# Down projections with seven block products for four of eleven 2x2 block groups, in a two-layer decoder trunk

## The chip, the cores and the metric

The kernel runs on one core of one Trainium2 chip. The metric is the device time of one execution in microseconds (us), lower is better. Each kernel is timed in several executions, and the median is given.

## What is computed

Two pre-norm decoder layers on 256 tokens of width 2048, all in float32: three groups of attention heads behind one input projection, an output projection `w_o`, and a gated MLP with a causal convolution. The change is in the MLP's last product:

```python
def _conv_gated_mlp(h, w_up, conv_w, conv_b, w_down):
    u = jnp.einsum('bsd,df->bsf', h, w_up)            # 2048 -> 2 x 5632
    u = lax.conv_general_dilated(u, conv_w[:, None, :], ...) + conv_b   # causal, width 3, per channel
    a, g = jnp.split(u, 2, axis=-1)
    return jnp.einsum('bsf,fd->bsd', jax.nn.silu(g) * a, w_down)        # 5632 -> 2048

for l in range(DEPTH):          # DEPTH = 2, D_FF = 5632, D_MODEL = 2048, SEQ = 256
    ...
    x = x + jnp.einsum('bsm,md->bsd', mix, w_o[l])
    h = _rmsnorm(x, ffn_norm[l])
    x = x + _conv_gated_mlp(h, ffn_w_up[l], ffn_conv_w[l], ffn_conv_b[l], ffn_w_down[l])
return _rmsnorm(x, final_norm)
```

## The kernel before

Every float32 value is split into two parts, `hi` (rounded to the format that TensorE multiplies fast) and `lo` (the rest), and a product is three matmuls: hi by hi, hi by lo, lo by hi.

**The weight stream.** All weights lie in HBM in the order in which they are used, as blocks of 128x128, 16 to a chunk (1 MB). `load` brings a chunk into one of three `raw` buffers with one DMA from the queue of SyncE. `convert(s)` turns half a chunk (eight blocks, 128x1024) into a `hi` tile, with a cast on ScalarE (line 140), and a `lo` tile, with a subtraction on VectorE (line 141). There are five `hi` and five `lo` buffers, so the conversion of a half-chunk waits until TensorE is done with the half-chunk five places earlier. `weights` calls `convert` for the half-chunk in use and the next two, the last with a higher priority (`AHEAD`, in places of program order).

**The MLP.** It runs in two halves of 22 column tiles of the inner width. For each tile the up projection makes two products over 16 blocks (`mm_t`, lines 195 and 200, each a PSUM bank of the three called `mm`), `total` adds the two parts of a bank (ScalarE line 269, VectorE line 271), and GpSimd, ScalarE and VectorE apply scale, convolution and gate (lines 834 to 842). `to_hl` splits the result into `hi` and `lo` in one `slot` tile (32 slots). Then `residual(acts, ...)` does the down projection of this half: for each of four column groups of 512 (`j`), `mm_v` goes over the 22 tiles; for each tile and each half of the 256 tokens (`t`) it issues three matmuls with the activations as the stationary operand (lines 251 to 253), and two `mm` banks collect the sums. At the end of a column group VectorE adds each bank to the residual `xr[t]` (line 471). In the second half of a layer the squares of the finished columns are summed on ScalarE (line 433) and, in layer 0, the columns are transposed on TensorE for the next layer (`RowNorm.turn`, line 442, PSUM banks `s`); in layer 1 GpSimd multiplies them by the final gain (line 863).

**What sets the order.** The queues of the engines are filled by a list scheduler when the program is built: it goes by priority (the order of the code, moved by `high_priority`) and by its own estimate of when operands are ready. At run time each queue is worked off in its order; an instruction that waits holds all behind it on its engine.

## Time and profile before

| | |
|---|---|
| median of 3 runs (lowest, highest) | 2248.11 us (2248.07, 2248.27) |
| the profiled execution, its own time | 2248.09 us |
| its span, from the first to the last instruction | 2246.3 us |
| granted TensorE clock, mean | 0.999 |
| TensorE busy | 2235.3 us, 12083 matmuls |
| VectorE, ScalarE, GpSimd busy | 1487.2, 1205.2, 404.3 us |
| weights and inputs read from HBM | 409.49 MB, 183 GB/s over the span |

In the profile, PE is TensorE, PEld its loading of stationary operands, DVE VectorE, ACT ScalarE, POOL GpSimd, SP the queue of SyncE. Matmuls are pipelined, so a matmul's recorded duration is longer than the time from one to the next. "idle before" is time in which an engine stood still ahead of an instruction, with the instruction that ended it.

### The profile page before, as it was taken

How to read it: one execution, taken by the hardware profiler on the slowest of the kernel's cores; microseconds unless marked ns; L12 is line 12 of the kernel's file. 1: busy time of each engine (PE TensorE's matmuls, PEld its weight loads, DVE VectorE, ACT ScalarE, POOL GpSimd, SP SyncE). 2: the span in 40 equal slices, each digit the busy share in tenths (PEclk: the TensorE clock that was granted, in tenths of full speed). 3: DMA queues.
4: the chain of work that ended last, by engine and by line, in shares of the span. 5: the costliest groups of instructions: out<-in, count | busy, mean ns of one | idle time of the engine just before them, and what ended most of it. 6: DMA issues, size and time to landing. Idle time of an engine off the chain costs nothing.

```text
span 2246.3 us, 31038 instructions
## 1 busy us (share of the span) xinstructions
PE 2235.3 (100%) x12083; PEld 1928.9 (86%) x12083; DVE 1487.2 (66%) x2318; ACT 1205.2 (54%) x1869; POOL 404.3 (18%) x395
## 2 busy tenths in 40 slices
PE   9999999999999999999999999999999999999998
PEld 8888978888888888888888889788888888888887
DVE  8767766677764577775574787566666646777654
ACT  7455645555543455554454566456555434555543
POOL 4600000222210022220040110003333101222210
PEclk9999999999999999999999999999999999999999
DMA  8544445455555555555555444354555555555653
GB/s 317 200 158 160 154 141 180 163 192 195 190 206 187 187 188 188 189 198 195 187 173 202 151 156 169 131 183 174 187 187 188 206 191 187 192 190 190 213 188 131
DMA packets 60915, 413.59 MB, mean 184 GB/s; under 512 B 6880, under 2 KB 7008, under 8 KB 11744
## 3 DMA queue, kind: packets, MB, share of 16 engines
q1 hardware_dynamic: 60336, 411.06, 51.8%
q8 instruction: 95, 1.56, 0.3%
q10 hardware_dynamic: 432, 0.55, 0.1%
q14 instruction: 52, 0.43, 0.1%
HBM read 409.49 MB, written 2.10 MB: 183 GB/s over the span
## 4 chain that ended last, share of the span: by engine, by line
PE 99%; ACT 1%; DMA 0%; DVE 0%; issue 0%; SPq 0%; ACTq 0%
PE mm L195 37%; PE mm L200 19%; PE mm L251 12%; PE mm L253 12%; PE mm L252 12%; PE s L483 2%; PE mm L234 1%; PE mm L776 1%; PE mm L777 1%; PE mm L778 1%; PE pv L515 1%; PE mm L232 0%; PE s L442 0%; PE misc L386 0%; PE pv L516 0%; ACT hi L140 0%
## 5 line engine op out<-in xcount | busy, mean ns | idle before, releaser
L141 DVE TENSOR_TENSOR lo<-raw,hi 128x1024 fp32r<-128x1024 f32 (+1 forms) x776 | 974.5, 1263 | 499.6 <-ACT hi L140 461.0
L140 ACT CAST hi<-raw 128x1024 fp32r<-128x1024 f32 (+1 forms) x776 | 800.6, 1039 | 475.7 <-PE mm L253 369.0
L195 PE MATMUL mm<-h,hi 128*128 128x512 f32 x3584 | 863.8, 392 | 0.0
L195 PEld LDWEIGHTS mm<-h,hi 128*128 128x128 f32 x3584 | 664.7, 188 | 135.5 <-ACT tmp L269 1.3
L200 PEld LDWEIGHTS mm<-h,lo 128*128 128x128 f32 x3584 | 460.6, 190 | 13.6
L200 PE MATMUL mm<-h,lo 128*128 128x256 f32 x3584 | 465.4, 283 | 0.0
L251 PE MATMUL mm<-hi,slot 128*128 128x512 f32 x992 | 387.8, 391 | 0.0
L253 PE MATMUL mm<-hi,slot 128*128 128x512 f32 x992 | 384.8, 388 | 0.0
L252 PE MATMUL mm<-lo,slot 128*128 128x512 f32 x992 | 384.7, 388 | 0.0
L834 POOL TENSOR_TENSOR tmp<-tmp,rstd 128x256 f32<-128x256 f32 x176 | 193.1, 1097 | 1037.9 <-DVE tmp L271 728.0
L837 ACT ACTIVATE tmp<-tmp,par 128x256 f32<-128x256 f32 x176 | 106.0, 602 | 311.6 <-POOL tmp L834 311.6
L251 PEld LDWEIGHTS mm<-hi,slot 128*128 128x128 f32 x992 | 186.3, 188 | 41.1 <-issue 4.0
L253 PEld LDWEIGHTS mm<-hi,slot 128*128 128x128 f32 x992 | 186.2, 188 | 38.5
L252 PEld LDWEIGHTS mm<-lo,slot 128*128 128x128 f32 x992 | 186.4, 188 | 36.8
L838 DVE SCALAR_TENSOR_TENSOR tmp<-tmp,par,tmp 128x255 f32<-128x255 f32 x176 | 84.5, 480 | 150.5 <-ACT tmp L837 150.5
L269 ACT COPY tmp<-mm 128x256 f32<-128x256 f32 (+1 forms) x233 | 85.7, 368 | 62.0 <-PE mm L195 34.0
L842 POOL TENSOR_TENSOR tmp<-tmp,tmp 128x256 f32<-128x256 f32 x88 | 75.5, 858 | 211.6 <-ACT tmp L841 209.3
L271 DVE TENSOR_TENSOR tmp<-mm,tmp 128x256 f32<-128x256 f32 (+1 forms) x233 | 97.3, 418 | 5.4 <-ACT tmp L269 5.1
L839 DVE SCALAR_TENSOR_TENSOR tmp<-tmp,par,tmp 128x254 f32<-128x254 f32 x176 | 85.0, 483 | 6.2
L841 ACT ACTIVATE tmp<-tmp 128x256 f32<-128x256 f32 x88 | 36.8, 418 | 61.7 <-DVE tmp L839 61.7
L251 PE MATMUL mm<-hi,h 128*128 128x512 f32 (+1 forms) x192 | 68.3, 356 | 0.0
L253 PE MATMUL mm<-hi,h 128*128 128x512 f32 (+1 forms) x192 | 67.9, 354 | 0.0
(196 smaller groups left out, 1469.8 us busy)
## 6 DMA issues: line engine op xcount, KB each, us to landing
raw<-in_w SPq DMA_DIRECT2D x381, 1024.0 KB, 4.8
raw<-in_w SPq DMA_DIRECT2D x14, 256.0 KB, 5.3
slot<-in_x SPq DMA_DIRECT2D x8, 256.0 KB, 5.1
x<-in_xn SPq DMA_DIRECT2D x2, 1024.0 KB, 10.9
out<-x SPq DMA_DIRECT2D x6, 256.0 KB, 2.6
slot<-in_fin SPq DMA_DIRECT2D x4, 256.0 KB, 6.2
out<-x ACTq DMA_DIRECT2D x2, 256.0 KB, 2.6
par<-in_par SPq DMA_DIRECT2D x1, 325.0 KB, 7.9
```

The lines of the kernel that those rows point to most:

```text
L140: nc.scalar.copy(hi[:, a], src[:, a])
L141: nc.vector.tensor_tensor(lo[:, a], src[:, a], f(hi[:, a]), ALU.subtract)
L195: nc.tensor.matmul(ps, ws[i][0], moving[i], start=(i == 0), stop=bool(flip and i == k - 1))
L200: nc.tensor.matmul(ps[:, :T], ws[i][1], moving[i][:, :T], start=False, stop=(not flip and i == k - 1))
L251: nc.tensor.matmul(ps[t][:, :n], s_hi, hi, start=(i == 0), stop=False)
L252: nc.tensor.matmul(ps[t][:, :n], s_hi, lo, start=False, stop=False)
L253: nc.tensor.matmul(ps[t][:, :n], s_lo, hi, start=False, stop=(i == k - 1))
L269: nc.scalar.copy(t[:rows], ps[:rows, T : 2 * T])
L271: nc.vector.tensor_tensor(u[:rows], ps[:rows, :T], t[:rows], ALU.add)
L834: nc.gpsimd.tensor_tensor(uu, u, rstd, ALU.mult)
L837: nc.scalar.activation(y, uu, AF.Identity, scale=q_[:, w + 2 : w + 3], bias=q_[:, w + 3 : w + 4])
L839: nc.vector.scalar_tensor_tensor(y[:, 2:], uu[:, : T - 2], q_[:, w : w + 1], y[:, 2:], ALU.mult, ALU.add)
```

## The change

The four column groups of a down projection are taken in pairs of groups (columns `c1`, `c2` of 512 each) and the 22 tiles in eleven pairs (`PAIRS`). For a pair of tiles the product is then a 2x2 by 2x2 product of blocks: two token halves by two tiles, and two tiles by two column groups. For the pairs 3, 6, 8 and 10 (`SEVEN`) it is computed with seven block products, by Strassen's identity in Winograd's form, and for the other seven pairs with eight as before. This is done for both pairs of column groups in the first half of each layer, and for the first pair in the second half: six passes over eleven pairs in all, called groups here. The second half's last two column groups stay as they were.

A chunk of a seven-product pair gives 3.5 half-chunks of converted weights where it gave 2: twelve of its blocks directly, and four sums of blocks, which `prepare` makes with three additions on VectorE (one of 128x1024, two of 128x512, buffers `sum`). The activations of such a pair are likewise combined (`seven_forms`: four subtractions and additions of 128x128 on GpSimd, then four splits instead of two). The products go to seven PSUM banks, with an eighth, `d`, for what only the eight-product pairs add to the second token half and `c2`. At the end of a group the banks are combined into the residual with eight VectorE instructions, one ScalarE copy and four GpSimd additions, where four VectorE additions stood. `step` now converts three half-chunks ahead instead of two, everywhere.

```diff
-AHEAD = 60
+AHEAD = 80
+PAIRS = HALF // 2
+SEVEN = (3, 6, 8, 10)
...
     def tmp():
-        return work.tile([P, T], F32, tag="tmp", name=nm("tmp"), bufs=15)
+        return work.tile([P, T], F32, tag="tmp", name=nm("tmp"), bufs=14)
...
+        if at in sevens:
+            bounds += [(c, 0, 4, 8), (c, 0, 12, 4), (c, 1, 0, 8), (c, 2, 0, 8)]
+        else:
+            bounds += [(c, 0, i, min(SUB, n - i)) for i in range(0, n, SUB)]
...
+    def prepare(s):
...
+        tc.keep_in_program_order(nc.vector.tensor_tensor(
+            t13.rearrange(g, q=2), r[:, 1024:2048].rearrange(g, q=2),
+            r[:, 0:512].rearrange(g, q=1).to_broadcast([P, 2, 512]), ALU.add,
+        ))
+        nc.vector.tensor_tensor(t24[:, :512], t13[:, :512], r[:, 1536:2048], ALU.add)
+        nc.vector.tensor_tensor(t24[:, 512:], t24[:, :512], r[:, 512:1024], ALU.add)
...
+        src = (sums[c][form - 1] if form else raws[c])[:, o : o + n * P]
...
+    def step(s):
+        convert(s)
+        convert(s + 1)
+        with tc.high_priority(offset=AHEAD):
+            convert(s + 2)
+            convert(s + 3)
+            load(bounds[s][0] + 1)
+            load(bounds[s][0] + 2)
+        return subs[s]
...
+    def down(acts, groups):
+        for g in range(groups):
...
+            tags = {"d": ("s", 2), 2: ("s", 2), 3: ("pt", 1), 4: ("pv", 1), 1: ("mm", 3), 5: ("mm", 3), 7: ("mm", 3), 6: ("misc", 1)}
...
+            def prod(m, x, w, last=False):
...
+                nc.tensor.matmul(banks[m], xh, hi, start=fresh, stop=False)
+                nc.tensor.matmul(banks[m], xh, lo, start=False, stop=False)
+                nc.tensor.matmul(banks[m], xl, hi, start=False, stop=last)
...
+                if p in SEVEN:
+                    last = p == SEVEN[-1]
+                    step(s)
+                    prod(2, part(a[0], 1), quad(s, 0), last)
+                    prod(1, part(a[0], 0), quad(s, 1), last)
+                    step(s + 1)
+                    prod(3, part(a[2], 1), quad(s + 1, 0), last)
+                    step(s + 2)
+                    prod(5, part(a[1], 0), quad(s + 2, 0), last)
+                    prod(7, part(a[2], 0), quad(s + 2, 1), last)
+                    step(s + 3)
+                    prod(6, part(a[1], 1), quad(s + 3, 0), last)
+                    prod(4, part(a[3], 1), quad(s + 3, 1), last)
+                else:
...     (two products each into "d", 3, 2 and 4)
+            add = nc.vector.tensor_tensor
+            with tc.high_priority(offset=AHEAD):
+                add(xr[1][:, c2], xr[1][:, c2], banks["d"], ALU.add)
+                u = slot()
+                nc.scalar.copy(u, banks[1])
+                add(xr[0][:, c1], xr[0][:, c1], banks[2], ALU.add)
+                add(xr[0][:, c2], xr[0][:, c2], banks[3], ALU.add)
+                nc.gpsimd.tensor_tensor(xr[0][:, c1], xr[0][:, c1], u, ALU.add)
+                v = slot()
+                add(v, banks[6], u, ALU.add)
+                add(u, banks[5], v, ALU.subtract)
+                add(v, banks[7], v, ALU.add)
+                nc.gpsimd.tensor_tensor(xr[0][:, c2], xr[0][:, c2], u, ALU.add)
+                add(u, banks[5], v, ALU.subtract)
+                nc.gpsimd.tensor_tensor(xr[1][:, c1], xr[1][:, c1], v, ALU.add)
+                add(xr[1][:, c1], xr[1][:, c1], banks[4], ALU.add)
+                nc.gpsimd.tensor_tensor(xr[1][:, c2], xr[1][:, c2], u, ALU.add)
...
+    def seven_forms(both):
...
+        sub = nc.gpsimd.tensor_tensor
+        sub(s1, x21, x22, ALU.subtract)
+        sub(s3, x11, x21, ALU.subtract)
+        sub(s2, s1, x11, ALU.subtract)
+        sub(s4, x12, s2, ALU.add)
...
             if half == 0:
-                residual(acts, 0)
+                residual(acts, 0, first=4)
             elif l < DEPTH - 1:
...
-                residual(acts, 0, norm.turn)
+                residual(acts, 0, norm.turn, first=2)
             else:
-                gf = [slot() for _ in range(4)]
+                gf = [big.tile([P, 2 * T], F32, tag=f"h{k}", name=nm("gf")) for k in range(4)]
...
-                residual(acts, 0, gain, 8)
+                residual(acts, 0, gain, 8, 2)
```

In the rows below, a number behind a name tells buffers of one kind apart; line numbers are those of the respective kernel. In the changed kernel line 182 is the subtraction of `convert`, line 323 that of `total`, lines 551 to 553 are the three matmuls of `prod`, and the lines of the group's end are 592 (bank `d`), 594 (the copy of bank 1 to `u`, on ScalarE), 595 and 596 (banks 2 and 3), 597 (GpSimd, `u` into `xr[0]`, `c1`), 599 (`v` from bank 6), 600 (`u` from bank 5), 601 (`v` from bank 7), 602 (GpSimd, `u` into `xr[0]`, `c2`), 603 (`u` from bank 5 again), 604 (GpSimd, `v` into `xr[1]`, `c1`), 605 (bank 4) and 606 (GpSimd, `u` into `xr[1]`, `c2`).

**Place A: between the two groups of a first half** (layer 0). VectorE before, at the end of the second column group; the `lo` tiles are the next column group's weights:

```order
L141 TENSOR_TENSOR lo_1303_6776<-raw_1297_6741,hi_1302_6775 128x1024
L141 TENSOR_TENSOR lo_1306_6794<-raw_1297_6741,hi_1305_6793 128x1024
L471 TENSOR_TENSOR x0_77<-x0_77,mm_1271_6583 128x512
L471 TENSOR_TENSOR x1_78<-x1_78,mm_1272_6584 128x512
L141 TENSOR_TENSOR lo_1308_6810<-raw_1304_6779,hi_1307_6809 128x1024
L141 TENSOR_TENSOR lo_1311_6828<-raw_1304_6779,hi_1310_6827 128x1024
```

VectorE now. `lo_1338` (ahead of these rows) is the last half-chunk of pair 10, `lo_1341` and `lo_1343` (also ahead) are those of the next group's pair 0, and the rows begin with pair 1's:

```order
L182 TENSOR_TENSOR lo_1345_6856<-raw_1339_6830,hi_1344_6855 128x1024
L182 TENSOR_TENSOR lo_1349_6881<-raw_1339_6830,hi_1348_6880 128x1024
L595 TENSOR_TENSOR x0_77<-x0_77,s_1266_6467 128x512
L596 TENSOR_TENSOR x0_77<-x0_77,pt_1263_6456 128x512
L599 TENSOR_TENSOR slot_1347_6871<-misc_1292_6590,slot_1346_6866 128x512
L182 TENSOR_TENSOR lo_1354_6901<-raw_1350_6884,hi_1353_6900 128x1024
L600 TENSOR_TENSOR slot_1346_6866<-mm_1288_6578,slot_1347_6871 128x512
L601 TENSOR_TENSOR slot_1347_6871<-mm_1289_6582,slot_1347_6871 128x512
L182 TENSOR_TENSOR lo_1358_6919<-raw_1350_6884,hi_1357_6918 128x1024
L603 TENSOR_TENSOR slot_1346_6866<-mm_1288_6578,slot_1347_6871 128x512
L605 TENSOR_TENSOR x1_78<-x1_78,pv_1267_6474 128x512
```

Two additions have become seven here (`d` was added earlier), with two conversions between them. TensorE before, over the same boundary: the next column group starts in two other banks at once.

```order
L252 MATMUL mm_1272_6584<-lo_1294_6722,slot_1240_6388 128x512
L253 MATMUL mm_1272_6584<-hi_1293_6721,slot_1240_6388 128x512
L251 MATMUL mm_1300_6773<-hi_1295_6737,slot_799_4057 128x512
L252 MATMUL mm_1300_6773<-lo_1296_6738,slot_799_4057 128x512
L253 MATMUL mm_1300_6773<-hi_1295_6737,slot_799_4057 128x512
```

TensorE now, 38 matmuls behind the group's last one; the third of these rows is the first matmul into bank 4 (`pv`) of the new group, and belongs to pair 0:

```order
L551 MATMUL s_1351_6886<-hi_1353_6900,slot_885_4505 128x512
L552 MATMUL s_1351_6886<-lo_1354_6901,slot_885_4505 128x512
L551 MATMUL pv_1356_6911<-hi_1342_6845,slot_801_4061 128x512
L552 MATMUL pv_1356_6911<-lo_1343_6846,slot_801_4061 128x512
L553 MATMUL pv_1356_6911<-hi_1342_6845,slot_801_4061 128x512
```

The scheduler has put other products of the pairs 0 to 2 ahead of those that go into bank 4.

**Place B: from the second group of a first half into the up projection of the second half.** VectorE before; `mm_1359` is the bank of the first product of the up projection:

```order
L141 TENSOR_TENSOR lo_1361_7157<-raw_1356_7123,hi_1360_7156 128x1024
L141 TENSOR_TENSOR lo_1364_7163<-raw_1356_7123,hi_1363_7162 128x1024
L471 TENSOR_TENSOR x0_77<-x0_77,mm_1330_6965 128x512
L471 TENSOR_TENSOR x1_78<-x1_78,mm_1331_6966 128x512
L141 TENSOR_TENSOR lo_1371_7210<-raw_1362_7160,hi_1370_7209 128x1024
L141 TENSOR_TENSOR lo_1374_7216<-raw_1362_7160,hi_1373_7215 128x1024
L271 TENSOR_TENSOR tmp_1366_7200<-mm_1359_7155,tmp_1365_7198 128x256
```

VectorE now; `mm_1437` is the bank of that first product. The second product of the up projection is written to the bank that line 601 reads here (`mm_1378`), and waits for it.

```order
L182 TENSOR_TENSOR lo_1439_7319<-raw_1428_7267,hi_1438_7318 128x1024
L182 TENSOR_TENSOR lo_1442_7325<-raw_1440_7322,hi_1441_7324 128x1024
L595 TENSOR_TENSOR x0_77<-x0_77,s_1355_6904 128x512
L596 TENSOR_TENSOR x0_77<-x0_77,pt_1352_6893 128x512
L599 TENSOR_TENSOR slot_1436_7308<-misc_1381_7027,slot_1435_7303 128x512
L600 TENSOR_TENSOR slot_1435_7303<-mm_1377_7015,slot_1436_7308 128x512
L182 TENSOR_TENSOR lo_1449_7372<-raw_1440_7322,hi_1448_7371 128x1024
L601 TENSOR_TENSOR slot_1436_7308<-mm_1378_7019,slot_1436_7308 128x512
L323 TENSOR_TENSOR tmp_1444_7362<-mm_1437_7317,tmp_1443_7360 128x256
L603 TENSOR_TENSOR slot_1435_7303<-mm_1377_7015,slot_1436_7308 128x512
L605 TENSOR_TENSOR x1_78<-x1_78,pv_1356_6911 128x512
```

The chain of the group's end now stands between the conversions and reaches past the first `total` of the up projection. On TensorE, outside the down projections, the order of the matmuls is the same as before.

More of the change, by code (lines that the diff above doesn't have):

```diff
@@ L64, in chunk_list, with seven_starts @@
     return out
+def seven_starts():
+    per = KT * 39 + 84 + 16 * KT + 3 * FT * KT
+    out = set()
+    for l in range(DEPTH):
+        for half in range(2):
+            at = l * per + KT * 39 + 84 + 16 * KT + half * 3 * HALF * KT + 2 * HALF * KT
+            out |= {at + (g * PAIRS + p) * CH for g in range(2 - half) for p in SEVEN}
+    return out
 @with_exitstack
@@ L130, in convert @@
             return
-        c, o, n = bounds[s]
+        c, form, o, n = bounds[s]
         load(c)
         o = o * P
-        src = raws[c][:, o : o + n * P]
+        src = (sums[c][form - 1] if form else raws[c])[:, o : o + n * P]
         hi = wpool.tile([P, SUB * P], F32R, tag="hi", name=nm("hi"), bufs=5)
@@ L148, in weights @@
         if o == 0:
-            convert(s)
-            convert(s + 1)
-            with tc.high_priority(offset=AHEAD):
-                convert(s + 2)
-                load(bounds[s][0] + 1)
-                load(bounds[s][0] + 2)
+            step(s)
         o *= P
@@ L275 @@
     cs = const.tile([P, C_W], F32, tag="cs", name="cs")
-    pint = work.tile([P, T], I32, tag="tmp", name="pint", bufs=15)
+    pint = work.tile([P, T], I32, tag="tmp", name="pint", bufs=14)
     xr = [big.tile([P, D], F32, tag=f"x{t}", name=f"x{t}") for t in range(2)]
@@ L464, in rows, with residual @@
             return rows
-    def residual(stat, every, after=None, lag=0):
-        for j in range(4):
+    def residual(stat, every, after=None, lag=0, first=0):
+        if first:
+            down(stat, first // 2)
+            if after:
+                for j in range(first):
+                    for t in range(2):
+                        norm.add(j, t)
+                    if j:
+                        after(j - 1)
+            flat = []
+            for p, a in enumerate(stat):
+                flat += [((a[0], 0), (a[3], 0)), ((a[0], 1), (a[3], 1))] if p in SEVEN else a
+            stat = flat
+        for j in range(first, 4):
             ps = mm_v(stat, 512, every, {2: (lambda: after(j - 1))} if after and j else {}, lag if j == 3 else 0)
@@ L821 @@
         for half in range(2):
-            acts = []
+            acts, waiting = [], []
             for i in range(HALF):
```

109 lines of the change are left out of this document (99 added, 10 removed).

## Prediction

> **What bounds the kernel now.** I read the page first, then the chain that ended last, TensorE's own waits, and the stages one by one. On the page's busy row TensorE is busy for the whole span; in the row of the chain, 99% of it is TensorE; in the view of waits, TensorE's list is three entries of about a microsecond. The windows are the down projection of layer 0's first half, that of layer 1's first half, and the end.
>
> ```profile
> PE 2235.3 (100%) x12083; PEld 1928.9 (86%) x12083; DVE 1487.2 (66%) x2318; ACT 1205.2 (54%) x1869; POOL 404.3 (18%) x395
> PE 99%; ACT 1%; DMA 0%; DVE 0%; issue 0%; SPq 0%; ACTq 0%
> PE pv L284 <- DVE small L286: 1.5, 1, 1.5
> PE mm L231 <- DVE h L407: 0.8, 1, 0.8
> PE misc L371 <- DVE slot L559: 0.8, 1, 0.8
> 638.00:760.00 122.00, 122.00 (x547) 101.36 (x546) 63.01 (x59) 48.85 (x50) 1.85 (x2) 1.00 0.57 200
> 1753.00:1873.00 120.00, 120.00 (x531) 99.38 (x530) 62.87 (x61) 49.29 (x51) 4.40 (x3) 1.00 0.56 201
> 2240.00:2247.00 7.00, 0.00 (x0) 0.00 (x0) 1.31 (x3) 1.74 (x3) 0.00 (x0) 0.53 0.40 150
> ```
>
> In a down projection TensorE never stands still (122.00 of 122.00), VectorE works half of the time (63.01), GpSimd hardly. So the time is the sum of the matmuls' slots, and the question is twofold: how many slots go, and what new waits TensorE gets. The slot is not the recorded duration (0.39 us), which overlaps the next. From two starts in the timeline, 33 matmuls apart, it is (2237.45 - 2229.97) / 33 = 0.2267 us:
>
> ```profile
> 2229.97 0.39 PE L251 MATMUL mm<-hi,slot 128*128 128x512 f32 x1
> 2237.45 0.39 PE L251 MATMUL mm<-hi,slot 128*128 128x512 f32 x1
> ```
>
> **What goes.** Six groups, four pairs each, one block product of three matmuls less: 72 matmuls x 0.2267 = 16.3 us. All of it lies on the path. An eight-product pair takes 24 x 0.2267 = 5.44 us, a seven-product pair 4.76, a group 252 x 0.2267 = 57.1.
>
> **What comes, and its prices.** Groups by line and form, then the timeline for what instructions cost in a row and against each other:
>
> ```profile
> L141 DVE TENSOR_TENSOR lo<-raw,hi 128x1024 fp32r<-128x1024 f32 x762 | 964.9, 1274 | 495.5 <-ACT hi L140 457.0 <-PE mm L200 36.8 <-issue 0.4
> L141 DVE TENSOR_TENSOR lo<-raw,hi 128x512 fp32r<-128x512 f32 x14 | 9.5, 687 | 4.0 <-ACT hi L140 4.0
> L140 ACT CAST hi<-raw 128x1024 fp32r<-128x1024 f32 x762 | 792.2, 1047 | 470.0 <-PE mm L253 369.0 <-PE mm L195 56.9 <-issue 20.3
> L352 DVE TENSOR_TENSOR slot<-slot,sinT 128x512 f32<-128x512 f32 x8 | 5.5, 692 | 0.5
> L354 DVE TENSOR_TENSOR slot<-slot,slot 128x512 f32<-128x512 f32 x8 | 5.5, 689 | 0.2
> L671 ACT ACTIVATE slot<-mm,rcol 128x512 f32<-128x512 f32 x12 | 8.0, 686 | 3.9 <-PE mm L253 3.9
> L521 DVE TENSOR_TENSOR slot<-tmp,slot 128x256 fp32r<-128x256 f32 x96 | 40.2, 419 | 28.2 <-ACT slot L520 28.2
> L842 POOL TENSOR_TENSOR tmp<-tmp,tmp 128x256 f32<-128x256 f32 x88 | 75.5, 858 | 211.6 <-ACT tmp L841 209.3 <-issue 2.3
> L863 POOL TENSOR_TENSOR x<-x,slot x6: 1289/1501/1712, 2150.3 to 2211.8; 128x512 f32<-128x512 f32 x6
> 695.50 1.22 DVE L141 TENSOR_TENSOR lo<-raw,hi 128x1024 fp32r<-128x1024 f32 x1 [1.49 <-ACT hi L140]
> 696.64 1.28 DVE L471 TENSOR_TENSOR x<-x,mm 128x512 f32<-128x512 f32 x2
> 1026.38 0.39 PE L253 MATMUL mm<-hi,slot 128*128 128x512 f32 x1
> 1026.81 1.05 ACT L140 CAST hi<-raw 128x1024 fp32r<-128x1024 f32 x1 [1.67 <-PE mm L253]
> 1027.89 1.23 DVE L141 TENSOR_TENSOR lo<-raw,hi 128x1024 fp32r<-128x1024 f32 x1 [1.50 <-ACT hi L140]
> 2150.32 2.97 POOL L863 TENSOR_TENSOR x<-x,slot 128x512 f32<-128x512 f32 x2 [26.04 <-ACT slot L433]
> 2152.42 1.95 DVE L141 TENSOR_TENSOR lo<-raw,hi 128x1024 fp32r<-128x1024 f32 x1 [1.54 <-ACT hi L140]
> 411.67 0.74 POOL L842 TENSOR_TENSOR tmp<-tmp,tmp 128x256 f32<-128x256 f32 x1 [3.61 <-ACT tmp L841]
> 411.82 0.42 DVE L271 TENSOR_TENSOR tmp<-mm,tmp 128x256 f32<-128x256 f32 x1 [0.92 <-ACT tmp L269]
> 790.58 1.92 PE mm L200 x16
> raw<-in_w SPq DMA_DIRECT2D x381, 1024.0 KB, 4.8
> ```
>
> A conversion lasts 1.23 us undisturbed, but the next VectorE instruction that depends on nothing begins 1.14 later (695.50 to 696.64); two PSUM additions last 1.28 together, so one lasts 0.68 and its place in the queue is 0.60. From a matmul's start to the cast that it releases go 0.43 us, which is 0.20 past its slot; then 1.05 for the cast and 0.03 to the subtraction. GpSimd's 128x512 addition: 1.29 alone. Against GpSimd, a VectorE instruction with two SBUF operands is held: the conversion at 2152.42 ended 1.08 us after GpSimd did (2154.37 against 2153.29). One that reads PSUM and SBUF is not: 411.82 took its usual 0.42 while GpSimd ran. I take it that GpSimd likewise waits for a conversion that has begun, and needs 1.1 more.
>
> *The sums of weights.* No row has a 128x1024 addition with a repeated operand. Nearest: line 141, 1.23, and line 352, which repeats an operand and costs the same as line 354, which doesn't (692 and 689 ns). I take 1.14 in the queue, and 0.61 for each addition of 512. A seven-product chunk then costs VectorE 3 x 1.14 + 0.61 + 1.14 + 2 x 0.61 = 6.4 us against TensorE's 4.76, a plain one 2.28 against 5.44. So VectorE falls behind by 1.6 in each seven-product pair and gains 3.2 in each plain one; over a group it needs 4 x 6.4 + 7 x 2.28 + 8 x 0.60 = 46.4 of 57.1 us. The five buffers carry the swing: stepping through pairs 8, 9 and 10 (below), the last half-chunk of pair 10 is ready 1.7 us before its use. Inside a group I cost the sums at nothing; that cover is gone if the three together cost 1.7 us more than these 2.4. ScalarE's 3.5 casts are 3.7 us, below TensorE's 4.76. Loads land in 4.8; each is issued at least 5.4 ahead.
>
> *The forms of activations.* In the up projection, 16 pairs get two more splits (2 x 0.42 on VectorE, 2 x 0.41 on ScalarE) and four small GpSimd operations (each below line 842's 858 ns). TensorE waits there for conversions alone, which run four half-chunks (11 us) ahead; nothing on the path. Pair 10's forms hold the conversions of pair 3 behind them, for a chain some 2 us longer than today's; by my count these are ready 9 us into the down projection, and wanted at 16.3.
>
> *Fourteen `tmp` buffers, the gain's loads, three half-chunks ahead.* One buffer of fifteen; the gain's DMA now waits on SP for the last up projection, with one weight load behind it that isn't due for 10 us: nothing.
>
> **The ends of the groups** are what remains. Let T be the slot behind the group's last matmul. VectorE's queue is determined from pair 9 on: the second conversion of that pair needs the buffer of pair 8's first two products, done at T - 4.76 - 5.44 - 4.76 + 1.36 = T - 13.6; with 0.20, 1.05 and 0.03 behind it, it starts at T - 12.3. Then come, with the prices above, pair 10's two conversions, the sum, line 592, the sum, a conversion, the sum, and 1.1 us of waiting for ScalarE's cast of that sum. `lo_1338` (and its like) starts at T - 4.1, the next three at -3.0, -1.8 and -0.7; the fourth at +0.8, since ScalarE copies bank 1 ahead of its cast. TensorE has these in time.
>
> *Place A, twice.* Line 595 starts at 1.9 and ends at 2.6, while TensorE wants bank 2 at 10 slots, 2.3: a wait of 0.4. Lines 596 and 599 to 3.8. GpSimd runs line 597 from 2.7 to 3.95 and holds `lo_1354`, which ends at 5.0. Line 600 to 5.6, 601 to 6.35. Line 602 on GpSimd, 5.7 to 6.95, holds `lo_1358` to 8.0, and that holds line 604 to 9.1. Line 605 ends at 9.9. TensorE reaches bank 4 after 38 slots, at 8.6. Sum: 1.3 us. Without any holding 0.4; with the full 1.23 and 0.68 for each place in the queue, and GpSimd's additions at 1.5, 3.0.
>
> *Place B, twice.* Here two conversions stand ahead of line 595 (3.1) and one between 600 and 601. Line 597 runs on GpSimd from 3.8 to 5.1; 600 to 5.8; `lo_1449` to 6.95; 601 to 7.55. The second product of the up projection wants that bank at 5.58 (16 x 0.2267 and the 16 narrower ones, 1.92 in the chain: 5.55). A wait of 2.0. From below 1.5; if GpSimd gets ahead of `lo_1449` and everything lasts its full time, 4.35.
>
> *Second half of layer 0, once.* Seven matmuls behind T, TensorE transposes columns of `c1`, which wait for line 597, at 2.5 against 1.6: 0.9 us, and later 0.1 for line 605. 1.0; bounds 0.5 and 2.5. *Of layer 1, once:* the third bank is wanted after 27 slots, 6.1; the final gain's GpSimd multiplication stands between lines 597 and 602 and delays line 601 to 6.4. 0.3; bounds 0 and 1.7.
>
> Sum: 2 x 1.3 + 2 x 2.0 + 1.0 + 0.3 = 7.9 us; from below 2 x 0.4 + 2 x 1.5 + 0.5 = 4.3, from above 2 x 3.0 + 2 x 4.35 + 2.5 + 1.7 = 18.9. I take 7.9, the value by the prices in a row, which the timeline shows for this very sequence.
>
> **The forecast.** The profiled execution took 2248.09 us (span 2246.3; the median, 2248.11, is the same within 0.02). 2248.09 - 16.3 + 7.9 = 2239.7 us, 0.37% faster; with the bounds of the waits 2236.1 and 2250.7. A measurement of this kernel can tell 0.2%, 4.5 us, from no change.
>
> **The rivals.**
>
> *The ends take most of the gain* (no change). The same mechanism with waits of 12 to 20 us: each wait hangs on a queue, so a delay that I missed ahead of T moves all six. For it: 1.5 us more at each end is enough (7.9 + 9 = 16.9, 2248.7). Against it: in the trace VectorE's starts follow these prices to 0.05 us. Chance 0.22.
>
> *The sums are dear* (slower). If the three additions cost 4.7 instead of 2.4 us a chunk, pair 10's come out 2.35 later, and so does every step behind T in all six groups: 7.9 + 6 x 2.35 = 22, 2253.8 us. It decides against the change from waits of 16.3, that is 1.4 us more a chunk, and shows as slower from 20.8, 2.15 more. For it: no row of that form. Against it: lines 352 and 354. Chance 0.07.
>
> *TensorE loses its speed in the waits.* At its start it is slow: eleven matmuls of zeros take 4.31 us, 0.39 each instead of 0.2267, 1.8 us lost.
>
> ```profile
> 1.45 4.31 PE L284 MATMUL pv<-slot 128*128 128x512 f32 x11 [1.45 <-DVE small L286]
> 0.00:12.00 12.00, 9.74 (x42) 7.86 (x43) 7.06 (x16) 8.62 (x18) 2.87 (x9) 1.00 0.82 286
> ```
>
> If each of the two waits at place B did that again, the time would be 2239.7 + 3.6 = 2243.3; if all six did, 2250.5. The granted clock in the window's row is 1.00 even in that first stretch, so it can't tell. The Trainium skill ("TensorE: Matmul & The Clock Gate", Part 1) has a rule that speaks against the change here: TensorE's clock falls to half after an idle window of about 3.4 us and comes back after one such window of work. By that rule none of my waits, at most 2.0 us in one piece, is long enough, and the sum stays 7.9. No run here yet shows a wait in the middle. Chance 0.04.
>
> *Fewer matmuls don't show.* The order has the 72 fewer, with the same three into one bank at a time; the slot can't change by more than it does between today's stages. Left out.
>
> **How the numbers follow.** Forecast, waits between 4 and 12 us: 0.67, all faster than 2243.8. Ends take it: 0.22, of which 0.04 end over +0.2%. Sums dear: 0.07, mostly slower. Clock: 0.04, half of it faster. So faster 0.68, same 0.22, slower 0.10. The range must leave out no more than 0.2: from 2235 (waits of 3) to 2250 (waits of 18). The forecast's own is 2236 to 2244.
>
> **What the profile after would show.** 72 matmuls less at an unchanged slot. TensorE's list of waits with `pv` for line 605 (about 1 us, twice), `mm` of the up projection for line 601 (2 us, twice), `s` for lines 595 and 597 (below 1), 8 us in all, each wait at a group's end. VectorE about 135 us busier (24 x 4.5, and the ends). No wait of TensorE for a `lo` tile inside a group: such waits would speak for dear sums. Wrong I would be above all if the queue of VectorE comes to T later than I count.

## The result, and the profile after

The changed kernel takes 2262.78 us (median of 4 runs, 2259.59 to 2266.26) against 2248.09 us (2248.01 to 2248.27) for the kernel before: ratio 1.0065, 95% interval 1.0053 to 1.0077. It is slower by 14.7 us. The forecast was 2239.7 us, the range 2235 to 2250. The profiled execution took 2264.71 us, its span is 2262.9 us.

From the page of the changed kernel, the busy row and the chain that ended last:

```profile
PE 2232.6 (99%) x12011; PEld 1921.7 (85%) x12011; DVE 1625.9 (72%) x2494; ACT 1247.8 (55%) x1955; POOL 470.9 (21%) x483
PE 55%; DVE 8%; ACT 3%; issue 2%; POOL 2%; ACTq 0%; DVEq 0%; POOLq 0%
```

The 72 matmuls are gone (12083 to 12011), yet TensorE is busy only 2.7 us less, and the chain, which was TensorE for 99%, now runs through VectorE, ScalarE and GpSimd too. TensorE's waits in the changed kernel (us in total, times, longest):

```profile
PE mm L248 <- DVE lo L182: 6.9, 7, 1.7
PE mm L243 <- DVE slot L601: 3.6, 2, 1.8
PE mm L551 <- ACT hi L181: 1.9, 2, 1.0
PE mm L552 <- DVE lo L182: 1.9, 2, 1.0
PE pv L551 <- DVE x L605: 1.6, 2, 0.8
...
PE s L494 <- POOL x L597: 1.0, 1, 1.0
...
PE pv L648 <- DVE tmp L881: 0.7, 1, 0.7
PE pv L648 <- ACT slot L643: 0.7, 1, 0.7
...
PE misc L423 <- DVE tmp L890: 0.6, 1, 0.6
PE mm L304 <- DVE lo L182: 0.3, 1, 0.3
```

Four kinds can be told apart. `slot` for line 601, `x` for 605 and 597, and line 304 are the groups' ends (line 304 stands behind the last group of layer 1, and waits for a converted half-chunk). Line 248 is the up projection, which waits for converted weights. Lines 551 and 552 wait for the first seven-product pair of a group. Lines 648 and 423 are in the attention, far from the change's products. And there is something that is no wait. The windows of the down projection and, inside it, of two stretches of 4 us (the eighth column from the start of a row is the granted clock):

```profile
640.00:760.00 120.00, 117.25 (x515) 96.05 (x514) 96.85 (x105) 60.72 (x71) 13.08 (x13) 0.99 0.55 194
667.00:671.00 4.00, 3.75 (x9) 2.96 (x10) 3.97 (x5) 3.98 (x5) 0.00 (x0) 0.57 0.75 264
672.00:676.00 4.00, 4.00 (x19) 3.31 (x18) 3.08 (x4) 1.35 (x2) 0.00 (x0) 1.00 0.95 369
```

From 667 to 671 the clock is 0.57 and 9 matmuls are done where 19 are done a little later. TensorE's timeline there:

```profile
664.47 0.39 PE L553 MATMUL pt<-hi,slot 128*128 128x512 f32 x1
665.79 0.50 PE L551 MATMUL mm<-hi,slot 128*128 128x512 f32 x1 [0.94 <-ACT hi L181]
667.25 0.75 PE L552 MATMUL mm<-lo,slot 128*128 128x512 f32 x1 [0.95 <-DVE lo L182]
...
668.23 0.63 PE L551 MATMUL mm<-hi,slot 128*128 128x512 f32 x1
668.65 0.63 PE L552 MATMUL mm<-lo,slot 128*128 128x512 f32 x1
...
670.77 0.39 PE L551 MATMUL pv<-hi,slot 128*128 128x512 f32 x1
671.00 0.40 PE L552 MATMUL pv<-lo,slot 128*128 128x512 f32 x1
```

After two waits of just under 1 us the slot, the time from one matmul's start to the next one's, is 0.427 us (0.42 from 668.23 to 668.65) until 670.77, then 0.23 again. The clock record has four such stretches of 3.41 us at half speed in this execution (from 578.6, 667.3, 1039.4 and 1896.1) and, in the kernel before, none until TensorE is done. Each costs 3.41 x (1 - 0.2267 / 0.427) = 1.6 us.

To add it all up, I took for each matmul the time from its start to the next one's, less the median of its kind (called slots lost below), and summed by stage; the table gives the difference to the kernel before, in us.

| stage | more than before | of it at half clock |
|---|---|---|
| attention, both layers | 3.8 | |
| up projections of layer 0 | 10.7 | 1.6 |
| first seven-product pair of layer 0's groups | 8.1 | 3.2 |
| ends of the groups | 10.4 | 1.6 |
| sum | 33.0 | 6.4 |
| 72 matmuls fewer | -16.3 | |
| difference | +16.7 (spans: 16.6) | |

Layer 1 loses nothing in its up projections and at its first seven-product pairs.

### The profile page after: what moved, and what is told of

It is laid out like the page before. It is cut to its first block, busy times and chain, and to the rows that moved or that the text cites. A ratio compares the mean times of both kernels' runs of the same rounds, so it can differ in the third digit from the quotient of the medians.

```text
span 2262.9 us, 31345 instructions
## 1 busy us (share of the span) xinstructions
PE 2232.6 (99%) x12011; PEld 1921.7 (85%) x12011; DVE 1625.9 (72%) x2494; ACT 1247.8 (55%) x1955; POOL 470.9 (21%) x483
## 4 chain that ended last, share of the span: by engine, by line
PE 55%; DVE 8%; ACT 3%; issue 2%; POOL 2%; ACTq 0%; DVEq 0%; POOLq 0%
PE mm L243 20%; PE mm L248 10%; DVE lo L182 5%; PE mm L303 4%; PE mm L304 4%; PE mm L305 4%; ACT hi L181 2%; PE s L553 1%; PE s L552 1%; PE s L551 1%; PE pv L551 1%; PE pv L552 1%; PE pv L553 1%; PE s L616 1%; POOL tmp L990 1%
## 5 line engine op out<-in xcount | busy, mean ns | idle before, releaser
L181 ACT CAST hi<-raw 128x1024 fp32r<-128x1024 f32 (+1 forms) x776 | 786.3, 1025 | 324.6 <-PE mm L305 160.8
L990 POOL TENSOR_TENSOR tmp<-tmp,rstd 128x256 f32<-128x256 f32 x176 | 165.3, 939 | 795.8 <-DVE tmp L323 482.2
L303 PE MATMUL mm<-hi,slot 128*128 128x512 f32 (+1 forms) x464 | 182.6, 394 | 0.0
L304 PE MATMUL mm<-lo,slot 128*128 128x512 f32 (+1 forms) x464 | 179.8, 388 | 0.3 <-DVE lo L182 0.3
L305 PE MATMUL mm<-hi,slot 128*128 128x512 f32 (+1 forms) x464 | 179.5, 387 | 0.0
L303 PEld LDWEIGHTS mm<-hi,slot 128*128 128x128 f32 x464 | 87.3, 188 | 21.0 <-issue 3.3
L305 PEld LDWEIGHTS mm<-hi,slot 128*128 128x128 f32 x464 | 87.3, 188 | 17.6
L304 PEld LDWEIGHTS mm<-lo,slot 128*128 128x128 f32 x464 | 87.3, 188 | 16.8 <-DVE lo L182 0.7
L181 ACT CAST hi<-sum 128x1024 fp32r<-128x1024 f32 x48 | 50.5, 1053 | 86.0 <-DVE sum L141 46.5
L1010 POOL TENSOR_TENSOR tmp<-tmp,tmp 128x256 f32<-128x256 f32 x56 | 49.9, 892 | 132.6 <-ACT tmp L997 132.6
L551 PE MATMUL s<-hi,slot 128*128 128x512 f32 x192 | 75.3, 392 | 0.1
L552 PE MATMUL s<-lo,slot 128*128 128x512 f32 x192 | 75.1, 391 | 0.0
```

The costliest lines, as they stand in the source:

```text
L181: nc.scalar.copy(hi[:, a], src[:, a])
L303: nc.tensor.matmul(ps[t][:, :n], s_hi, hi, start=(i == 0), stop=False)
L304: nc.tensor.matmul(ps[t][:, :n], s_hi, lo, start=False, stop=False)
L305: nc.tensor.matmul(ps[t][:, :n], s_lo, hi, start=False, stop=(i == k - 1))
L551: nc.tensor.matmul(banks[m], xh, hi, start=fresh, stop=False)
L552: nc.tensor.matmul(banks[m], xh, lo, start=False, stop=False)
```

## The experiments

My theory after the result ("forms"): combining and splitting the activations holds back the casts of weights, and so causes the second and third row of the table. Its rivals: the conversions' new order (three ahead), or the sums of weights.

**First round.** *two_forms* leaves out the combining and two of the four splits; *three_ahead* is the kernel before with that part of the change alone; *raw_sums* leaves out the sums; *layer1_only* leaves layer 0 as it was.

```diff
# two_forms
-        sub(s1, x21, x22, ALU.subtract)
...
-        for src, n in ((v[:, :, 0], 2), (e[:, :T], 2), (e[:, T:], 2), (v[:, :, 1], 2)):
+        for src, n in ((v[:, :, 0], 2), (v[:, :, 1], 2)):
# three_ahead, against the kernel before
-AHEAD = 60
+AHEAD = 80
...
                 convert(s + 2)
+                convert(s + 3)
# raw_sums
-        nc.vector.tensor_tensor(t24[:, :512], t13[:, :512], r[:, 1536:2048], ALU.add)
-        nc.vector.tensor_tensor(t24[:, 512:], t24[:, :512], r[:, 512:1024], ALU.add)
-        sums[c] = (t13, t24)
+        sums[c] = (r[:, :1024], r[:, 1024:2048])
# layer1_only
-                residual(acts, 0, first=4)
+                residual(acts, 0, first=4 * l)
```

> The changed kernel, but a seven-product pair's activations are not combined: the four GpSimd subtractions and two of the four splits are left out, and the plain splits stand in for all four forms (so the sums it computes are others). Theory 'forms': in the changed kernel's profile TensorE loses 10.6 us in layer 0's up projections and 8.1 us at the first seven-product pair of layer 0's groups, because the forms push back the casts of the weights; without them both go: 2262.8 - 18.7 = 2244 us (2241 to 2247). Rival 'three ahead' (the conversions' new order causes these waits): 2258 to 2264. Rival 'dear sums': 2258 to 2264.

> The kernel before, with only the changed kernel's conversion three half-chunks ahead (and AHEAD = 80 and fourteen tmp buffers); eight products everywhere. Theory 'forms': only the waits in the attention that the changed kernel shows (0.8 + 0.9 + 1.3 us) come: 2251 us (2249 to 2253), TensorE waits nowhere in the up projections. Rival 'three ahead': the waits of the up projections come here too: 2256 to 2264.

> The changed kernel without the three VectorE additions of each seven-product chunk: unsummed blocks stand in for the sums of weights (so the products are others). Theory 'forms': the waits at the first seven-product pair of layer 0 (8.1 us) and most of those at the groups' ends (10.3 us) go, since VectorE comes there 2.4 us or more earlier, while the 10.6 us in layer 0's up projections stay: 2246 us (2243 to 2251). Rival 'dear sums': nearly all of the 33 us of lost time go: 2232 to 2238.

> Seven products in layer 1 alone; layer 0's down projections as in the kernel before (three half-chunks ahead and AHEAD = 80 stay everywhere). Theory 'forms': layer 1's conversions run 6 us ahead in its up projections and swallow the forms; saved 36 x 0.2267 = 8.2 us, lost 3 us in the attention and about 5 us at layer 1's groups' ends: 2248 us (2245 to 2251). Rival 'three ahead': layer 0's up projections wait as in the changed kernel, 10 us more: 2258.

Measured, with the ratio to the kernel before on the same chip: two_forms 2247.27 us (0.9993, 0.9984 to 1.0003); three_ahead 2251.67 (1.0013, 1.0004 to 1.0023); raw_sums 2253.83 (1.0024, 1.0014 to 1.0034); layer1_only 2248.11 (0.9998, 0.9989 to 1.0008). In two_forms no wait of the up projections (line 248) and none of the first seven-product pairs is left; its waits begin with the ends:

```profile
PE mm L243 <- DVE slot L601: 3.9, 2, 2.1
PE pv L551 <- DVE x L605: 1.6, 2, 0.8
```

So without the forms those two rows go: the median is 15.5 us below the changed kernel's (forecast 18.7, and 0.3 us above the range). three_ahead has only the attention's part, as expected. raw_sums missed, with 9 us won instead of 17: the first pairs' waits went and place B's nearly did, but the up projections kept 12.4 us and place A its 1.5 us each. That speaks against sums that are dear everywhere, as the rival had it (2232 to 2238). It also shows that the second row and the third differ: the up projections need only the forms, while the waits at the first seven-product pairs go if either the forms or the sums are taken out, so they take both. layer1_only came out as worked out: 8.2 us won, the ends and the attention lost.

**Second round: where the forms act, a mended order, and the clock.**

```diff
# early_subs
-                        waiting.append(both)
+                        waiting.append(seven_subs(both))
...
-                    acts[i // 2 - 1] = seven_forms(waiting.pop())
+                    acts[i // 2 - 1] = seven_splits(*waiting.pop())
# old_ahead; deep is 1 in down() and 0 elsewhere
-            convert(s + 3)
+            if deep[0]:
+                convert(s + 3)
# early_old_3579: both of these, and
-SEVEN = (3, 6, 8, 10)
+SEVEN = (3, 5, 7, 9)
# four_buffers, against the kernel before (lo alike)
-        hi = wpool.tile([P, SUB * P], F32R, tag="hi", name=nm("hi"), bufs=5)
+        hi = wpool.tile([P, SUB * P], F32R, tag="hi", name=nm("hi"), bufs=4)
```

> The changed kernel with the four GpSimd subtractions of a seven-product pair issued as soon as the pair's second tile is done, instead of one tile later, directly ahead of the splits that read them. Theory 'GpSimd in the queue': what pushes the casts of the weights back is above all that ScalarE's split of the forms stands in its queue and waits 1.5 us for GpSimd (1.53 in the trace at 564.97); with the results there in time the 10.6 us in layer 0's up projections shrink to 3 or less, and the 8.1 us at the first seven-product pair to 4 to 8: 2252 us (2247 to 2257). Rival 'splits': the two more splits themselves take the lead (0.8 us on ScalarE and on VectorE a pair), and the time stays at 2259 to 2266.

> The changed kernel with the conversions two half-chunks ahead and AHEAD = 60 outside the down projections, as in the kernel before; three and 80 only within them. Theory 'forms': the three waits in the attention go (3 us), the up projections and the ends stay about as they are: 2259.5 us (2255 to 2263). Rival: three ahead is what keeps the lead in the up projections at all, and with two the waits there grow: over 2266.

> The two edits above together, and seven products for the pairs 3, 5, 7 and 9 instead of 3, 6, 8 and 10, so that a plain pair ends each group: banks 1, 5, 6 and 7 are complete 5.4 us ahead of the group's last matmul, and no forms stand at the end of the up projections. Saved 16.3 us as before; lost by my theory nothing in the attention, at most 4 us in the up projections, at most 4 at the ends and 1 elsewhere: 2239 us (2234 to 2246). Rival 'the queue's order decides': the ends of the groups stay behind the same conversions and cost 8 to 12 us: 2246 to 2252.

> The kernel before with four instead of five hi and lo buffers, so that TensorE waits often, and for different lengths. It tests the clock. Theory 'idle share': the granted clock falls to half for one window of 3.41 us (a fixed grid) whenever TensorE stood idle for 1.6 us or more of the window before, in one piece or several, and not up to 1.3 us; each such window costs about 1.6 us. Rival: only a wait that fills a whole window does it, and the clock stays at 1.00 unless a wait exceeds 3.4 us. The Trainium skill (TensorE: Matmul & The Clock Gate, Part 1) gives this second rule. Time: slower than before, 2255 to 2400 us.

Measured: early_subs 2262.40 (1.0062, 1.0047 to 1.0077); old_ahead 2265.01 (1.0072, 1.0057 to 1.0087); early_old_3579 2262.44 (1.0060, 1.0043 to 1.0077); four_buffers 2252.11, one run. All four missed. early_subs tested nothing: the scheduler had put the subtractions and the splits at the same place before, and ScalarE still waits 1.52 us there. old_ahead took the attention's waits away, but with two half-chunks ahead in the up projections TensorE waits there longer, and now at the first seven-product pairs of layer 1 as well: layer 1 needs three ahead from its up projections on. early_old_3579 inherits both, and at place A bank 4 is now 1.6 us late, since what was line 605 and the second use of `u` wait for GpSimd there; place B lost its wait. four_buffers hardly made TensorE wait (0.85 us of listed waits at most in any 3.41 us) and no half clock came, which fits both rules and decides nothing.

**Third round: GpSimd or the splits.** The prices of the four subtractions in the changed kernel, by line and form:

```profile
L664 POOL TENSOR_TENSOR slot<-slot,slot 128x128 f32<-128x128 f32 x16 | 18.2, 1141 | 1.3
L663 POOL TENSOR_TENSOR slot<-slot 128x128 f32<-128x128 f32 x16 | 14.3, 893 | 1.3
L662 POOL TENSOR_TENSOR slot<-slot 128x128 f32<-128x128 f32 x16 | 12.6, 785 | 1.2
L665 POOL TENSOR_TENSOR slot<-slot,slot 128x128 f32<-128x128 f32 x16 | 7.4, 461 | 1.3
```

Together 3.3 us a pair, where undisturbed (0.46 each) they would be 1.8: VectorE's conversions hold three of the four.

```diff
# four_splits
-        sub(s1, x21, x22, ALU.subtract)
...
-        for src, n in ((v[:, :, 0], 2), (e[:, :T], 2), (e[:, T:], 2), (v[:, :, 1], 2)):
+        for src, n in ((v[:, :, 0], 2), (both[:, :T], 2), (both[:, T:], 2), (v[:, :, 1], 2)):
# late_splits
-            nc.scalar.copy(h, src)
+            tc.keep_in_program_order(nc.scalar.copy(h, src))
# v2: late_splits, SEVEN = (3, 5, 7, 9), three ahead from the up projection on, and in down()
                 add(xr[1][:, c2], xr[1][:, c2], banks["d"], ALU.add)
+                add(xr[0][:, c2], xr[0][:, c2], banks[3], ALU.add)
+                add(xr[0][:, c1], xr[0][:, c1], banks[2], ALU.add)
+                add(xr[1][:, c1], xr[1][:, c1], banks[4], ALU.add)
                 u, v = slot(), slot()
...
-                nc.gpsimd.tensor_tensor(xr[0][:, c1], xr[0][:, c1], u, ALU.add)
+                add(xr[0][:, c1], xr[0][:, c1], u, ALU.add)
# v2_layer1: v2 with layer 0 as in layer1_only
```

> The changed kernel without the four GpSimd subtractions of a seven-product pair, but with all four splits (two of them of uncombined activations, so the products are others). Theory 'GpSimd in the queue': ScalarE's second split no longer waits 1.5 us for GpSimd, and most of the 10.6 us in layer 0's up projections and of the 8.1 us at its first seven-product pairs goes: 2250 us (2247 to 2254). Rival 'splits': the work of the two more splits, 0.8 us on ScalarE and on VectorE a pair, is what eats the lead: 2258 to 2265.

> The changed kernel with each split of the forms pinned on ScalarE behind what the code issues before it, so that it stands one tile (11 us) behind GpSimd's subtractions instead of directly behind them; nothing else is changed, and all the work is done. In the order the splits of the first pair now stand one tile later (early_subs had left the order of ScalarE as it was). Theory 'GpSimd in the queue': the 10.6 us in the up projections fall to 4 or less; pair 10, whose forms come at the end, keeps 4 to 8 us at the first seven-product pair: 2255 us (2251 to 2259). Rival 'splits': no change, 2259 to 2266.

> A version meant to be faster than both: late splits; three half-chunks ahead only in the MLP, two in the attention; seven products for the pairs 3, 5, 7, 9; at a group's end the four banks that the next group wants first (d, 3, 2, 4) are added first, and the four additions of GpSimd are VectorE's. Saved 16.3 us; lost by my theory 0 in the attention, 2 to 4 in the up projections, 2 at the first seven-product pairs, 4 to 5 at the ends: 2241 us (2236 to 2248). Rival 'splits': 8 to 10 us stay in the up projections: 2248 to 2252.

> The version above in layer 1 alone, where the conversions run 4 to 6 us ahead; layer 0 as in the kernel before. Saved 8.2 us; lost 2 to 3 at the ends, nothing in the up projections by either theory: 2242.5 us (2240 to 2246).

Measured: four_splits 2250.20 (1.0007, 0.9997 to 1.0016); late_splits 2265.22 (1.0074, 1.0059 to 1.0089); v2 2249.96 (1.0006, 0.9996 to 1.0015); v2_layer1 2240.42 (0.9965, 0.9952 to 0.9978). v2_layer1 came out in its range, 8 us below the kernel before; v2 missed (2241 forecast), with 13 us of slots lost in layer 0's up projections. four_splits shows that GpSimd's subtractions are the larger part. In the changed kernel they act where I said, through ScalarE: its second split waits 1.53 us for GpSimd, the copy for the next tile's sum (line 321) stands behind it, and so the sum (line 323) and the scaling of that tile (line 990) are late:

```profile
564.97 0.41 ACT L674 CAST slot<-slot 128x256 fp32r<-128x256 f32 x1 [1.53 <-POOL slot L664]
565.28 0.36 ACT L321 COPY tmp<-mm 128x256 f32<-128x256 f32 x1
565.67 0.42 DVE L323 TENSOR_TENSOR tmp<-mm,tmp 128x256 f32<-128x256 f32 x1 [1.06 <-ACT tmp L321]
566.18 0.86 POOL L990 TENSOR_TENSOR tmp<-tmp,rstd 128x256 f32<-128x256 f32 x1 [0.70 <-DVE tmp L323]
```

late_splits shows that this is not the only way: ScalarE's splits of the combined blocks now stand some 10 us behind the subtractions and wait for nothing there, and the time is what it was. Its timeline at the same place:

```profile
562.97 0.46 POOL L662 TENSOR_TENSOR slot<-slot 128x128 f32<-128x128 f32 x1
563.51 1.32 POOL L664 TENSOR_TENSOR slot<-slot,slot 128x128 f32<-128x128 f32 x1
564.43 0.41 DVE L323 TENSOR_TENSOR tmp<-mm,tmp 128x256 f32<-128x256 f32 x1
564.77 1.21 DVE L182 TENSOR_TENSOR lo<-raw,hi 128x1024 fp32r<-128x1024 f32 x1
564.90 1.39 POOL L665 TENSOR_TENSOR slot<-slot,slot 128x128 f32<-128x128 f32 x1
566.26 0.74 POOL L990 TENSOR_TENSOR tmp<-tmp,rstd 128x256 f32<-128x256 f32 x1
567.03 0.60 ACT L993 ACTIVATE tmp<-tmp,par 128x256 f32<-128x256 f32 x1 [2.80 <-POOL tmp L990]
567.54 1.98 ACT L181 CAST hi<-raw 128x1024 fp32r<-128x1024 f32 x2
```

The next tile's sum (line 323) is there at 564.84. Its scaling (line 990) starts at 566.26, behind the subtractions on GpSimd, of which the last, held by the conversion at 564.77, takes 1.39 instead of 0.46 us. ScalarE's line 993 waits for it 2.80 us, and two casts of weights stand behind line 993. So with the wait on ScalarE gone, GpSimd's own queue holds the scaling, 1.4 us at this place, and it starts no earlier than before (566.26 against 566.18).

**Fourth round.** Taking that away, in two ways:

```diff
# subs_after: late_splits, and (pinned in this place)
                     nc.gpsimd.tensor_tensor(uu, u, rstd, ALU.mult)
+                    if j == 0 and waiting:
+                        waiting.append(seven_subs(waiting.pop()))
# subs_vector: late_splits, and
-        sub = nc.gpsimd.tensor_tensor
+        sub = nc.vector.tensor_tensor
# v3 and v3_vector: v2 with the one and with the other
```

> As late_splits, but GpSimd's four subtractions of a seven-product pair are pinned behind the next tile's first scaling (the multiplication by rstd) on GpSimd, where they stood ahead of it. Theory 'GpSimd's own queue': that scaling is no longer 1.4 us late in each seven-product pair, and of the waits in layer 0's up projections (5.8 us in the first half and 2.9 in the second in late_splits) at most 2 us stay; the first seven-product pair keeps its wait, since pair 10's forms have no next tile: 2256 us (2252 to 2260). Rival 'port': GpSimd's subtractions hold VectorE's conversions wherever they stand, and the time stays at 2262 to 2266.

> As late_splits, with the four subtractions on VectorE instead of GpSimd (four small instructions of 128x128 a pair, about 0.25 us each by half of the 0.42 us of a 128x256 one). Theory 'GpSimd's own queue': the chain behind GpSimd goes, 1 us of VectorE comes: the waits in the up projections fall to 3 us or less and that at the first seven-product pairs by half: 2254 us (2250 to 2259). Rival 'any work in the up projection costs lead': 2260 to 2266.

> The version v2 with the subtractions behind the next tile's first scaling. In v2's trace all that TensorE lost against the kernel before is 17.2 us in layer 0's up projections and first seven-product pairs. Theory 'GpSimd's own queue': most of it goes (no pair 10 here): 2237 us (2233 to 2242). Rival 'port': 2248 to 2251.

> The version v2 with the subtractions on VectorE. Theory 'GpSimd's own queue': 2238 us (2233 to 2243). Rival 'any work in the up projection costs lead': 2247 to 2251.

Measured: subs_after 2259.23 (1.0051, 1.0033 to 1.0069); subs_vector 2259.98 (1.0051, 1.0035 to 1.0067); v3 2245.01 (0.9984, 0.9975 to 0.9994); v3_vector 2249.36 (1.0005, 0.9995 to 1.0015). The direction is right: behind the scaling the subtractions cost 6 and 5 us less, on VectorE 5 and 1. The 6 are in part the clock's: in the profiled executions the up projections lose 3.6 us less than in late_splits, and two half-clock stretches are gone. From v2 to v3, without such stretches in either, they lose 4.2 less. But the second row of the table did not go, v3 missed its forecast of 2237, and v3_vector came out where its rival, "any work in the up projection costs lead", had it. In v3 TensorE's longest entry is still

```profile
PE mm L250 <- DVE lo L182: 6.1, 12, 0.9
```

all in layer 0's up projections, and there VectorE's version (v3_vector, 14 us of slots lost) costs as much as GpSimd's (v2, 13). That left the question how much room there is at all.

To see it, I matched each conversion with the first matmul that reads its `lo` tile, and took as its lead the time from the one's end to the other's start. The least lead of a tile, once the first few tiles of each up projection are past and in the last one, in us:

| | layer 0, 1st half | layer 0, 2nd half | layer 1, 1st half | layer 1, 2nd half |
|---|---|---|---|---|
| before | 1.6 to 2.9 | 5.1 to 5.1 | 4.6 to 2.0 | 6.0 to 6.0 |
| after | 1.5 to 0.1 | 4.7 to 0.1 | 6.0; 4.3 at a pair, then back | the same |
| two_forms | 1.5 to 0.3 | 4.8 to 3.4 | 6.0 | 6.0 |
| four_splits | 1.5 to 0.1 | 5.1 to 1.2 | 6.0 | 6.0 |

In layer 0 each seven-product pair costs 0.5 us of lead in two_forms, 1.2 in four_splits and 2.8 in the changed kernel (the next pair there takes the 2.0 that are left), and it does not come back from tile to tile (by 0.1 us at most) while TensorE does not wait. In layer 1 it costs 1.7 and comes back by 0.5 a tile. *slow_chain* adds a known piece of work to the kernel before:

```diff
                 nc.scalar.activation(ys[1], ys[1], AF.Silu)
+                nc.scalar.copy(ys[1], ys[1])
```

> The kernel before with one ScalarE copy of 128x256 in place (0.37 us) added to each tile of the up projections, behind the SiLU. ScalarE is busy 54% of the time. Theory 'no slack in the loop': in the kernel before, the least lead of the conversions rises by 0.1 us a tile in layer 0's first half and falls by 0.15 a tile in layer 1's first half; with 0.37 more, they fall by 0.3 and 0.5, the leads of 1.6 and 4.6 us are gone after some tiles, and TensorE waits 4 and 6 us there: 2255 us (2251 to 2260). Rival 'idle engines have room': 2248 to 2249.5.

Measured: 2290.77 us (1.0187, 1.0170 to 1.0204). TensorE's waits in its four up projections, one window each (none in the fourth, layer 1's second half, where the lead stays at 6.0 until the last four tiles and ends at 3.5):

```profile
PE mm L200 <- DVE lo L141: 8.2, 14, 0.6
PE mm L200 <- DVE lo L141: 7.9, 13, 0.9
PE mm L200 <- DVE lo L141: 8.3, 14, 0.7
```

With one copy more a tile, on an engine that is busy 54% of the time, the lead falls by 0.8 us a tile in three up projections, and once it is gone TensorE loses 0.85 us a tile. The rival "idle engines have room" is out there. The size was far over what I expected (2255). Where some of the 0.8 comes from can be read in its trace: GpSimd's multiplication behind the copy now meets a conversion and lasts 1.41 us (median) instead of 0.74 in the kernel before, and the next tile's scaling stands behind it on GpSimd. At the starts of the down projections TensorE waits 5.7 us more.

## Why the prediction was wrong

**Right: the saving.** 72 matmuls less at an unchanged slot, 16.3 us.

**Right: the ends, at five of six places.** Forecast 7.9 us of waits; the list has 3.6 for line 601 (2.0 each forecast, 1.8 measured), 1.6 for line 605 (0.9 each; 0.8) and 1.0 for line 597 (1.0). By the slots lost, which hold the short waits too, the six places cost 8.8, and 1.6 more from one half-clock stretch. This working, by places in VectorE's queue, held. At the sixth place, layer 1's second half, the 0.3 agrees by luck: I had TensorE wait for the bank that line 601 frees, and it waited for a conversion that GpSimd had held (line 304).

**Right: the price of the sums.** 2.4 us a chunk forecast, by places in the queue. By line and form in the changed kernel:

```profile
L141 DVE TENSOR_TENSOR sum<-raw 128x1024 f32<-128x1024 f32 x24 | 29.3, 1219 | 0.0
L145 DVE TENSOR_TENSOR sum<-sum,raw 128x512 f32<-128x512 f32 x24 | 16.6, 691 | 0.6
```

With two of the second kind (lines 145 and 146) that is 2.6 us of duration, the price of the like instructions in the kernel before. Pair 10's last half-chunk in the first group was ready 1.6 us before its use (forecast 1.7), and VectorE is 138.7 us busier (135). What did not hold is "inside a group I cost the sums at nothing": at layer 0's first seven-product pairs TensorE waits for `lo` tiles, and raw_sums, without the sums, has no such wait. By the prediction's own sign that spoke for dear sums; their price shows that the cover was missing, not that they cost more.

**Wrong, first: "The forms of activations", "TensorE waits there for conversions alone, which run four half-chunks (11 us) ahead; nothing on the path".** This step failed, and it is worth 10.7 us and, together with the sums, 8.1 more of the 33.0. The 11 us was what five buffers allow; what the queues give is 1.6 to 5.1 us in layer 0. It stood in the trace of before. Its rows in layer 0, at 566 us:

```profile
566.18 0.42 ACT L841 ACTIVATE tmp<-tmp 128x256 f32<-128x256 f32 x1 [1.13 <-DVE tmp L839]
566.51 1.04 ACT L140 CAST hi<-raw 128x1024 fp32r<-128x1024 f32 x1
...
567.58 1.23 DVE L141 TENSOR_TENSOR lo<-raw,hi 128x1024 fp32r<-128x1024 f32 x1 [1.49 <-ACT hi L140]
```

The cast stands behind the SiLU on ScalarE, which waits for VectorE, which waits for ScalarE and GpSimd. Its `lo`, ready at 568.81, is read from 571.34: 2.5 us ahead, not 11. The same place in the changed kernel:

```profile
575.11 0.42 ACT L997 ACTIVATE tmp<-tmp 128x256 f32<-128x256 f32 x1 [1.13 <-DVE tmp L995]
575.43 1.03 ACT L181 CAST hi<-raw 128x1024 fp32r<-128x1024 f32 x1
...
576.49 1.23 DVE L182 TENSOR_TENSOR lo<-raw,hi 128x1024 fp32r<-128x1024 f32 x1 [1.48 <-ACT hi L181]
...
577.77 1.45 PE L248 MATMUL mm<-h,lo 128*128 128x256 f32 x8 [1.72 <-DVE lo L182]
```

The order is the same; everything on ScalarE is later, and TensorE waits 1.72 us. The count for pair 10's forms (pair 3 ready at 9 us, wanted at 16.3) failed by the same step: layer 0 enters its down projections with a lead of about 0.1 us, and the count started from one that was not there. How much of the 8.1 us is pair 10's own is not shown: v2 and v3, with no forms at the end of the up projections, still lose 3.9 and 3.6 us at those places, against 4.9 in the changed kernel without the half-clock stretches.

**Wrong, second: "three half-chunks ahead, everywhere: nothing".** three_ahead, that part alone, takes 3.0 us more than the kernel before on the same chip (2248.68), all in the attention, where VectorE's copy for the next product now stands behind one more conversion.

**Wrong, third: the clock.** I gave it 0.04, and by the rule that I cited no wait was long enough. The Trainium skill (TensorE: Matmul & The Clock Gate, Part 1) has the clock halve after an idle window of about 3.4 us; the trace disagrees: waits of 0.94 and 0.95 us close together did it. It cost 6.4 us in the profiled execution. The Trainium skill's other statement there, that the window is 3413 ns and runs free of the kernel, the traces bear out: the stretches start 88.75 and 372.05 us apart, 26.0 and 109.0 times 3.413, and the grid lies otherwise in each execution (the full clock came 4.5 to 7.5 us after the first instruction).

The rival that came nearest by its number was "the sums are dear" (2253.8); its mechanism, sums dearer than counted, was not there.

**What the cause is, and what stays open.** Shown by removal: without the forms the waits of the second and third row go (two_forms); without GpSimd's part of them most go (four_splits); with GpSimd's part moved, 6 us go, with the clock's share in them (subs_after); with work added that has nothing to do with the change the same waits come (slow_chain). Open is why layer 1's loop recovers its lead and layer 0's does not. The code is the same; the order that the scheduler gave differs, and I tried no other order.

v2_layer1 is faster than both: 2240.42 us, 0.35% under the kernel before. In it TensorE waits only where it did before the change:

```profile
PE pv L338 <- DVE small L340: 1.5, 1, 1.5
PE misc L425 <- DVE slot L718: 0.8, 1, 0.8
PE mm L281 <- DVE h L461: 0.5, 1, 0.5
```

It has the saving where the lead is (layer 1, 8.2 us), no forms at the end of an up projection, a plain pair and VectorE alone at the groups' ends, and the old order in the attention.

## What to carry to other kernels

Before work is added to an engine that "is idle half of the time", measure how far ahead of the bottleneck its results are, stage by stage, from the end of the producing instruction to the start of the first reader, and whether that lead comes back after a disturbance; buffers only tell the most that it can be. In-order queues that feed each other in a ring can be full at 54% busy. And count each new wait of TensorE at its length and, where a wait or several together take about 2 us out of 3.4, reckon with up to 1.6 us on top.

## What was new about the hardware

The granted clock halves for 3.41 us after a window of the same length, on a fixed grid, in which TensorE was busy for too small a share. In all 19 traces of this study (kernels before, after and the 17 others), with each matmul counted at the median slot of its kind (0.2267 us for 512 columns and 0.12 for 256 in the products with weights), the 15 windows in mid-kernel with a share up to 0.419 were all followed by a half-clock stretch, and none of those from 0.427 up was. So about 2 us of lost slots out of 3.41 are enough, in one wait (one listed as 1.72 us costs 1.97 us of slots) or in several. Since the grid is not tied to the kernel, it is chance whether a wait of this size is punished: of the two waits at place B (1.79 and 1.82 us), only the second was in the changed kernel's trace, and only the first in late_splits'. That fits the spread of the changed kernel's runs, 6.7 us with mean clocks from 0.995 to 0.999, against 0.3 us before.
